# Gate-over-sum scaling of the attention's probabilities moved to GpSimd, and the order made anew

## The chip, the core and the metric

The kernel runs on one core of a Trainium2 chip. The metric is the device time of one execution in microseconds (us). Engines are named as the profile names them: PE is TensorE's matrix multiplication, PEld its weight load, DVE is VectorE, ACT is ScalarE, POOL is GpSimd, SP is SyncE, which issues the transfers.

## What is computed

One decoder block on 512 tokens of width 1024. A normalised input is projected; half of the columns go through an RWKV-7 recurrence of 8 heads, the other half through sparse attention with 8 query heads; both halves meet in an output projection, and a gated feed-forward layer and a norm follow. The attention has three branches. Two of them, the selected blocks and the window, come out for 512 tokens as two causal softmaxes over keys of their own, each weighted by a gate. Cut to what matters here:

```
gates = sigmoid(gl)                                  # (token, head, branch)
ss = einsum(q, k_sel) * scale; p_s = softmax(mask(ss))
sw = einsum(q, k_win) * scale; p_w = softmax(mask(sw))
o  = gates[0] * o_c + gates[1] * (p_s @ v_sel) + gates[2] * (p_w @ v_win)
h  = x + concat(o_rwkv, o) @ w_out
```

## The kernel before, in words

The kernel is written as a recording: methods of `Kern` call engine operations, `Program.add` keeps each as an `Op` with its buffers, and nothing is issued yet. `Program.layout` then derives who depends on whom, `Program.schedule` puts all operations of all engines into one order, and `Program.issue` (line 560 emits every instruction, so all rows of the profile have that line) writes them out in it. Each engine runs its own instructions strictly in that order. The scheduler is a list scheduler: it keeps a clock for each engine, gives each operation a duration by `Program.cost` and a rank (the longest chain of such durations behind it, plus a bonus by stage from the table `PRIO`), and starts at each step the ready operation of highest rank on the engine that is free first.

`Kern.copy` and `Program.copy` record an operation that may run on DVE or ACT; the scheduler takes the engine that would be done first. A copy with a third argument multiplies each row by a scale: on DVE it is a TENSOR_SCALAR, on ACT an ACTIVATE.

The attention (`attention`, `probs`) runs over 16 heads as the text below counts them: 4 pairs of query heads times 2 branches times 2 heads. `probs` does one of them. For each of four row tiles of 128 tokens (i = 0 to 3, with 128, 256, 384 and 512 columns of keys), PE multiplies queries and keys (two matmuls), DVE masks, scales and takes the row extreme (the profile's CUSTOM_DVE_ANT_0, ISA in the order's rows), ACT takes the exponential and the row sum. Then DVE takes the reciprocal of the four sums and multiplies it by the gate: this 128x4 factor is what the four tiles are scaled by:

```
nv.reciprocal(st[:, 3], st[:, 2])
nv.tensor_tensor(st[:, 3], st[:, 3], gt[:, :, h, br + 1], op=A.mult)
for i in range(NT):
    self.nc.copy(P[i], P[i], st[:, 3, i:i + 1])
```

In `attention` PE transposes the scaled tiles 128x128 at a time, DVE or ACT copies them out of PSUM, and PE multiplies them with the values. Three sets of tiles P (`PBUFS`) go round: a fourth head's masking waits until the first one's transpositions are done. Beside the attention PE works on the last of four RWKV pairs (`rw_chain`, a serial chain of small matmuls with a copy on DVE or ACT after each), later on the first part of the output projection (`wout`).

GpSimd only sets memory to constants in this kernel. The transfers are all issued by SP.

Of the kernel before, what the change touches and what calls it, by code (L numbers as in the profile page):

```python
# [12 lines left out]
A = mybir.AluOpType  # L13
# [58 lines left out]
def size(x):  # L72
    return math.prod(x.shape[1:])
# [115 lines left out]
class Program:  # L189
# [94 lines left out]
    def cost(self, op):  # L284

        psum = any(isinstance(x.buf.key, str) for x in op.r)
        if op.eng == "tensor":
            if op.name == "transpose":
                return size(op.w[0]) * 2 / 2.4 + 2.5
            x = op.kw["rhs"]  # L290
            n, m = size(x), size(op.kw["lhsT"])
            p = 1 if x.dtype == R32 and n >= 256 else 2 if x.dtype == R32 else 4
            return p * max(n, m) / 2.4 + (5 if n <= 128 else 105) if p == 4 else p * max(n, m) / 2.4 + 13.5
        if op.eng == "sync":
            return 475
        if op.name == "preload_act_table_set":
            return 1300
        n = max(size(x) for x in op.r + op.w)
        column = (n > 1 or op.name == "scalar_tensor_tensor") and any(size(x) == 1 for x in op.r)
        if op.eng == "scalar":  # L300
            t = 50 + 0.84 * n if psum else 94 + 0.832 * n
            return t + 93 * column + 94 * ("accum_out" in op.kw)
        if op.eng == "gpsimd":
            return 40 + 0.8 * n if op.name == "memset" else 470
        if op.name == "reciprocal":
            return 66 + 6.2 * n
        fast = op.name in ("tensor_scalar", "tensor_copy") and not psum
        return 66 + 63 * column + n / (1.92 if fast else 0.96)
# [267 lines left out]
class Kern:  # L576
# [829 lines left out]
    def probs(self, h, br):  # L1406

        self.go("probs")
        nc, at = self.nc, self.att
        nv = nc.vector  # L1410
        gt = self.gate.rearrange("p i (h b) -> p i h b", b=3)
        st = self.tl(at, [128, 4, 4], "st", bufs=3)
        P = []
        for i in range(NT):
            n = 128 * (i + 1)
            nn = max(n, 256)
            pt = self.ps("d")
            for x in range(2):
                self.mm(pt[:, :nn], self.qT[h][:, i * 128:(i + 1) * 128], self.kT[br, h // 4, x][:, :nn], x == 0, x == 1)
            pr = self.tl(at, [128, n], f"P{i}", bufs=self.PBUFS)  # L1420
            nv.tensor_tensor_reduce(pr, pt[:, :n], self.cc[:, C_CAUS + 512 - n:C_CAUS + 512], -0.125, -NEG,
                                    op0=A.add, op1=A.min, accum_out=st[:, 1, i:i + 1])
            self.act(pr, pr, AF.Exp, scale=-1.0, bias=st[:, 1, i:i + 1], accum_out=st[:, 2, i:i + 1])
            P.append(pr)
            yield
        nv.reciprocal(st[:, 3], st[:, 2])
        nv.tensor_tensor(st[:, 3], st[:, 3], gt[:, :, h, br + 1], op=A.mult)
        for i in range(NT):
            self.nc.copy(P[i], P[i], st[:, 3, i:i + 1])
        return P  # L1430

    def attention(self):
# [515 lines left out]
```

## Time and profile before

| | us |
|---|---|
| median of 3 runs | 746.78 (746.73 to 747.71) |
| the profiled execution | 746.66 |
| its span, from the first instruction to the last | 744.8 |

The profile shows that one execution. Times in it are us, counted from the start of the span. Its views are read so:
- the page's first part has, for each engine, the busy time, its share of the span and the number of instructions;
- the view by stretches has the stretch and its length, then for each engine busy us with the number of instructions, the granted share of PE's clock, the share of the DMA engines and GB/s;
- the view of waits has the engine and what it waited for: us in total, times, the longest;
- the view by forms groups instructions of one shape: engine, operation, written<-read (s is SBUF, ps is PSUM), sizes, count, busy us and mean ns of one, then idle us of that engine just before them and what ended the idle;
- the timeline has start, duration, engine, operation, sizes and count of merged rows, and in brackets idle time before them.

A matmul's duration holds its way through the array, so that rows overlap: the spacing of matmuls is less than their mean duration.

### The profile page before, as it was taken

To read this page: it belongs to the slowest core of one execution; us is meant where nothing else is said; L and a number is where in the kernel's file an instruction comes from. 1 tells how busy PE (TensorE), PEld (TensorE's weight loads), DVE (VectorE), ACT (ScalarE), POOL (GpSimd) and SP (SyncE) were. 2 spreads that over 40 slices of the span, in tenths; PEclk is the share of its full clock that TensorE was granted. 3 is DMA by queue.
4 is the path that set the end of the run, shared out by engine and by line. 5 is a ranking of instruction groups with operands and counts; after the bars stand their busy time and mean duration, and the time that the engine had idled before them with its cause. 6 is when DMAs were issued, how large, how long until landed. Compare 5 with 4: busy or idle time off the path is not lost. (4 is left out here: it accounts for less than half of the span.)

```text
span 744.8 us, 14644 instructions
## 1 busy us (share of the span) xinstructions
PE 713.2 (96%) x5540; PEld 606.7 (81%) x5540; DVE 620.0 (83%) x1480; ACT 429.9 (58%) x948; POOL 3.7 (1%) x39
## 2 busy tenths in 40 slices
PE   5999999999989989999999999999999999999996
PEld 4988975768768666666788999999999999888785
DVE  6956988986997999798538999999999994687886
ACT  6555466554554688898336566565555552533545
POOL 0000000000000000000000000000000000000000
PEclk9999999999999999999999999999999999999999
DMA  8222326202110010533311233333333307464453
GB/s 318 72 77 62 98 78 199 75 27 74 41 31 28 16 45 1 170 103 96 114 57 71 72 114 114 114 120 108 114 100 114 101 22 258 159 216 149 139 171 116
DMA packets 39829, 77.37 MB, mean 104 GB/s; under 512 B 4432, under 2 KB 8912, under 8 KB 39760
## 3 DMA queue, kind: packets, MB, share of 16 engines
q1 hardware_dynamic: 39760, 76.45, 31.5%
q8 instruction: 43, 0.70, 0.4%
q14 instruction: 26, 0.21, 0.1%
HBM read 72.24 MB, written 4.19 MB: 103 GB/s over the span
## 5 line engine op out<-in xcount | busy, mean ns | idle before, releaser
L560 PE MATMUL ps<-s,s 128*128 128x256 f32 (+11 forms) x5412 | 710.4, 304 | 25.2 <-DVE s L560 19.1
L560 PEld LDWEIGHTS ps<-s,s 128*128 128x128 f32 (+5 forms) x5412 | 604.0, 170 | 130.2 <-DVE s L560 37.9
L560 DVE TENSOR_TENSOR s<-s,s 128x512 fp32r<-128x512 f32 (+18 forms) x662 | 378.4, 607 | 38.0 <-ACT s L560 18.9
L560 ACT ACTIVATE s<-s 128x512 fp32r<-128x512 f32 (+9 forms) x395 | 237.3, 619 | 226.7 <-DVE s L560 87.0
L560 ACT ACTIVATE s<-ps 128x256 f32<-128x256 f32 (+9 forms) x286 | 103.4, 376 | 43.2 <-PE ps L560 39.7
L560 DVE TENSOR_TENSOR s<-ps,s 128x256 f32<-128x256 f32 (+5 forms) x174 | 86.2, 506 | 29.7 <-PE ps L560 28.5
L560 ACT ACTIVATE s<-s,s 128x512 f32<-128x512 f32 (+4 forms) x142 | 72.1, 526 | 26.3 <-DVE s L560 25.0
L560 DVE COPY s<-ps 128x256 f32<-128x256 f32 (+6 forms) x77 | 32.4, 429 | 6.7 <-PE ps L560 5.4
L560 DVE CUSTOM_DVE_ANT_0 s<-ps,s 128x384 f32<-128x384 f32 (+3 forms) x64 | 29.8, 484 | 3.9 <-PE ps L560 3.7
L560 DVE SCALAR_TENSOR_TENSOR s<-s,s,s 128x512 f32<-128x512 f32 (+2 forms) x32 | 19.4, 630 | 13.8 <-DMA s<-in_n1w 6.6
L560 ACT ACTIVATE s<-ps,s 128x512 f32<-128x512 f32 (+1 forms) x34 | 20.1, 621 | 12.8 <-PE ps L560 12.6
L560 DVE SCALAR_TENSOR_TENSOR s<-ps,s,s 64x64 f32<-64x64 f32 (+1 forms) x62 | 23.9, 385 | 4.1 <-PE ps L560 1.5
L560 DVE CAST s<-s 128x512 fp32r<-128x512 f32 (+6 forms) x27 | 10.9, 409 | 14.5 <-PE ps L560 10.4
L560 DVE TENSOR_SCALAR s<-s,s 128x128 f32<-128x128 f32 (+4 forms) x67 | 21.4, 353 | 1.4 <-ACT s L560 0.8
L560 DVE STREAM_SHUFFLE s<-s 128x8 f32<-128x8 f32 (+14 forms) x60 | 14.0, 234 | 0.1
L560 ACT ACTIVATION_READ_ACCUMULATOR s<-s,s 128x1 f32 x64 | 12.1, 190 | 0.0
L560 DVE SCALAR_TENSOR_TENSOR s<-s,s 128x128 f32<-128x128 f32 (+1 forms) x26 | 8.9, 347 | 0.4
L560 ACT ACT_TABLE_LOAD x6 | 7.7, 1283 | 0.8 <-PEq L1935 0.7
L560 DVE TENSOR_TENSOR_SCAN s<-s,s 128x512 f32<-128x512 f32 x4 | 4.9, 1219 | 1.9 <-ACT s L560 1.9
L560 DVE COPY s<-s 64x512 f32<-64x512 f32 (+3 forms) x16 | 5.2, 323 | 0.8 <-PE ps L560 0.5
L560 DVE CAST s<-ps 128x512 fp32r<-128x512 f32 x7 | 4.8, 682 | 0.6 <-PE ps L560 0.6
L560 DVE DVE_READ_ACCUMULATOR2_ANT s<- 128x1 f32 x64 | 5.2, 82 | 0.0
(19 smaller groups left out, 41.2 us busy)
## 6 DMA issues: line engine op xcount, KB each, us to landing
s<-in_ffn_w SPq DMA_DIRECT2D x90, 256.0 KB, 2.7
s<-in_ffn_w SPq DMA_DIRECT2D x34, 512.0 KB, 3.8
s<-in_w_in_r SPq DMA_DIRECT2D x28, 256.0 KB, 2.7
s<-in_x SPq DMA_DIRECT2D x8, 512.0 KB, 5.4
s<-in_cw SPq DMA_DIRECT2D x16, 256.0 KB, 3.3
s<-in_w_out SPq DMA_DIRECT2D x8, 512.0 KB, 3.5
s<-in_w_in_n SPq DMA_DIRECT2D x8, 256.0 KB, 2.7
scr<-s SPq DMA_DIRECT2D x4, 512.0 KB, 2.6
```

The costliest lines, as they stand in the source:

```text
L560: ins = f(*[real(x) for x in op.args], **{k: real(x) for k, x in op.kw.items()})
```

## The change

Two lines. The four scalings of each head become TENSOR_SCALAR instructions of GpSimd, in place. The scheduler's cost of a GpSimd operation that is not a memset goes from a constant to one by its columns; no other such operation stands in the kernel, so this is the cost of the scalings alone: 392, 584, 776 and 968 in its nanoseconds.

```diff
         if op.eng == "gpsimd":
-            return 40 + 0.8 * n if op.name == "memset" else 470
+            return 40 + 0.8 * n if op.name == "memset" else 200 + 1.5 * n
...
         nv.tensor_tensor(st[:, 3], st[:, 3], gt[:, :, h, br + 1], op=A.mult)
         for i in range(NT):
-            self.nc.copy(P[i], P[i], st[:, 3, i:i + 1])
+            nc.gpsimd.tensor_scalar(P[i], P[i], st[:, 3, i:i + 1], None, op0=A.mult)
         return P
```

With these the scheduler makes another order. It is the same up to the first scalings, and again from the middle of the output projection on; the order of the transfers is the same throughout.

**DVE, where the first two heads are scaled.** s_2679 and s_2684 hold the two heads' sums and factors, s_287 the gates; s_2678, s_2748, s_2931, s_3026 are the first head's four tiles, s_2753, s_2945, s_3034 three of the second's. ps_63 belongs to the RWKV chain. Before:

```order
L560 RECIPROCAL s_2679<-s_2679 128x4
L560 TENSOR_TENSOR s_2679<-s_2679,s_287 128x4
L560 TENSOR_SCALAR s_2678<-s_2678,s_2679 128x128
L560 COPY s_1207<-ps_63 128x128
L560 TENSOR_SCALAR s_3026<-s_3026,s_2679 128x512
L560 TENSOR_SCALAR s_2931<-s_2931,s_2679 128x384
L560 TENSOR_SCALAR s_2748<-s_2748,s_2679 128x256
L560 RECIPROCAL s_2684<-s_2684 128x4
L560 COPY s_947<-ps_63 64x64
L560 TENSOR_TENSOR s_2684<-s_2684,s_287 128x4
```

In the changed kernel:

```order
L560 RECIPROCAL s_2679<-s_2679 128x4
L560 TENSOR_TENSOR s_2679<-s_2679,s_287 128x4
L560 COPY s_1207<-ps_63 128x128
L560 RECIPROCAL s_2684<-s_2684 128x4
L560 TENSOR_TENSOR s_2684<-s_2684,s_287 128x4
L560 COPY s_947<-ps_63 64x64 x2
```

The chain's copies and the second head's factor move up by the scalings that stood ahead of them.

**POOL, the same two heads, in the changed kernel.** Before, nothing follows the memsets there. s_2683 is the second head's smallest tile.

```order
L560 MEMSET s_71 64x64 x4
L560 ISA
L560 TENSOR_SCALAR s_3026<-s_3026,s_2679 128x512
L560 TENSOR_SCALAR s_2931<-s_2931,s_2679 128x384
L560 TENSOR_SCALAR s_2678<-s_2678,s_2679 128x128
L560 TENSOR_SCALAR s_2748<-s_2748,s_2679 128x256
L560 TENSOR_SCALAR s_3034<-s_3034,s_2684 128x512
L560 TENSOR_SCALAR s_2945<-s_2945,s_2684 128x384
L560 TENSOR_SCALAR s_2683<-s_2683,s_2684 128x128
L560 TENSOR_SCALAR s_2753<-s_2753,s_2684 128x256
```

All 64 scalings stand in one queue, a head's four in a row, the widest first. The ISA row, which selects GpSimd's library of operations, is new too.

**PE, ahead of the fourteenth head's transpositions.** s_881 holds the keys, s_2729 and s_2733 queries of the last two heads; s_78 is the identity, so rows that read it are transpositions; s_2612 and s_2702 are parts of the output projection's left side; s_2683, s_2753, s_2945, s_3034 the fourteenth head's tiles. Before:

```order
L560 MATMUL ps_65<-s_2928,s_2651 64x512 x2
L560 MATMUL ps_62<-s_881,s_2729 128x512
L560 MATMUL ps_58<-s_881,s_2733 128x512
L560 MATMUL ps_62<-s_881,s_2729 128x512
L560 MATMUL ps_58<-s_881,s_2733 128x512
L560 MATMUL ps_61<-s_3683,s_2612 128x512
L560 MATMUL ps_59<-s_78,s_2683 128x128
L560 MATMUL ps_59<-s_78,s_2753 128x128
```

In the changed kernel:

```order
L560 MATMUL ps_63<-s_2928,s_2651 64x512 x2
L560 MATMUL ps_59<-s_881,s_2729 128x512
L560 MATMUL ps_61<-s_881,s_2733 128x512
L560 MATMUL ps_59<-s_881,s_2729 128x512
L560 MATMUL ps_61<-s_881,s_2733 128x512
L560 MATMUL ps_65<-s_78,s_3034 128x128
L560 MATMUL ps_58<-s_3614,s_2612 128x512
L560 MATMUL ps_62<-s_3631,s_2612 128x512
L560 MATMUL ps_58<-s_3631,s_2612 128x512
L560 MATMUL ps_64<-s_78,s_2945 128x128
L560 MATMUL ps_64<-s_78,s_3034 128x128
L560 MATMUL ps_60<-s_78,s_2683 128x128
```

Three output projection matmuls and the transpositions of the wider tiles now stand ahead of the first transposition of the smallest tile, where one projection matmul stood.

## Rows read from the trace of the kernel before

**Rows 1.** The page's first part: busy time by engine.
```profile
PE 713.2 (96%) x5540; PEld 606.7 (81%) x5540; DVE 620.0 (83%) x1480; ACT 429.9 (58%) x948; POOL 3.7 (1%) x39
```

**Rows 2.** View by stretches: the attention's, and one of the feed-forward layer.
```profile
270.00:366.00 96.00, 93.29 (x596) 62.24 (x596) 83.39 (x274) 78.28 (x217) 0.00 (x0) 1.00 0.28 91
...
500.00:550.00 50.00, 50.00 (x419) 50.00 (x418) 47.30 (x84) 29.23 (x59) 0.00 (x0) 1.00 0.33 106
```

**Rows 3.** Waits of PE's weight load in the stretch 270 to 366.
```profile
PEld ps L560 <- DVE s L560: 10.1, 18, 1.3
...
PEld ps L560 <- ACT s L560: 5.6, 13, 0.8
```

**Rows 4.** View by forms, 270 to 366: scaling on DVE, scaling and exponential on ACT.
```profile
L560 ACT ACTIVATE s<-s,s 128x512 f32<-128x512 f32 x22 | 15.6, 714 | 0.4 <-DVE s L560 0.3
L560 ACT ACTIVATE s<-s,s 128x384 f32<-128x384 f32 x21 | 12.4, 606 | 1.2 <-DVE s L560 1.2
...
L560 ACT ACTIVATE s<-s,s 128x128 f32<-128x128 f32 x24 | 9.3, 395 | 1.9 <-DVE s L560 1.7
L560 ACT ACTIVATE s<-s,s 128x256 f32<-128x256 f32 x17 | 8.5, 502 | 1.1 <-DVE s L560 0.9
...
L560 DVE TENSOR_SCALAR s<-s,s 128x512 f32<-128x512 f32 x10 | 4.8, 481 | 0.0
...
L560 DVE TENSOR_SCALAR s<-s,s 128x256 f32<-128x256 f32 x12 | 4.1, 346 | 0.0
L560 DVE TENSOR_SCALAR s<-s,s 128x384 f32<-128x384 f32 x9 | 3.7, 415 | 0.0
...
L560 DVE TENSOR_SCALAR s<-s,s 128x128 f32<-128x128 f32 x11 | 3.1, 282 | 0.1
```

**Rows 5.** Timeline, 344 to 346.4: the fourteenth head's factor, scalings and first transposition.
```profile
344.37 0.15 DVE L560 TENSOR_TENSOR s<-s,s 128x4 f32<-128x4 f32 x1
...
344.79 1.23 DVE L560 TENSOR_TENSOR s<-s,s 128x1024 fp32r<-128x1024 f32 x1 [0.26 <-ACT s L560]
...
345.86 0.79 ACT L560 ACTIVATE s<-s,s 128x128 f32<-128x128 f32 x2
345.93 0.81 DVE L560 TENSOR_SCALAR s<-s,s 128x512 f32<-128x512 f32 x2
...
346.30 0.33 PE L560 MATMUL ps<-s,s 128*128 128x128 f32 x1 [0.29 <-ACT s L560]
```

**Rows 6.** Timeline, 270 to 275: the first head's factor and its last three scalings.
```profile
273.12 0.17 DVE L560 TENSOR_TENSOR s<-s,s 128x4 f32<-128x4 f32 x1
...
273.73 1.07 DVE L560 TENSOR_SCALAR s<-s,s 128x512 f32<-128x512 f32 x3
```

**Rows 7.** Timeline, 343 to 353: the last two heads' factors, and their scalings on DVE.
```profile
350.28 0.24 DVE L560 TENSOR_TENSOR s<-s,s 128x4 f32<-128x4 f32 x2
350.48 1.54 DVE L560 TENSOR_SCALAR s<-s,s 128x512 f32<-128x512 f32 x5
```

**Rows 8.** View by forms, whole span: GpSimd's memsets, and DVE's scan.
```profile
L560 DVE TENSOR_TENSOR_SCAN s<-s,s 128x512 f32<-128x512 f32 x4 | 4.9, 1219 | 1.9 <-ACT s L560 1.9
...
L560 POOL MEMSET s<- 128x1 f32 x19 | 1.6, 105 | 144.4 <-DVE s L560 144.1 <-POOLq L1935 0.3
...
L560 POOL MEMSET s<- 64x64 f32 x8 | 1.2, 145 | 19.1 <-PE ps L560 18.9
```

**Rows 9.** Timeline of GpSimd, 200 to 400: its last work.
```profile
224.02 0.35 POOL L560 MEMSET s<- 64x64 f32 x2 [18.93 <-PE ps L560]
```

**Rows 10.** View by forms, 270 to 366: DVE's instructions with two SBUF inputs.
```profile
L560 DVE TENSOR_TENSOR s<-s,s 128x1024 fp32r<-128x1024 f32 x8 | 9.7, 1213 | 0.3 <-ACT s L560 0.3
...
L560 DVE TENSOR_TENSOR s<-s,s 128x512 fp32r<-128x512 f32 x9 | 5.8, 685 | 1.6 <-ACT s L560 1.0 <-PE ps L560 0.6
...
L560 DVE TENSOR_TENSOR s<-s,s 128x4 f32<-128x4 f32 x16 | 2.4, 158 | 0.1
```

**Rows 11.** Timeline, 366 to 410: PE in the output projection.
```profile
365.79 42.36 PE L560 MATMUL ps<-s,s 128*128 128x512 f32 x234
```

## Prediction

> **What bounds the kernel now.** The page's first part says where to look: PE is busy 96% of the span, DVE 83%, POOL 1% [rows 1]. So the engine that gets the work has nearly nothing to do, and the end moves only as far as PE's waits do. The view by stretches says what is special about the attention: from 270 to 366 PE is busy 93.29 of 96 us, DVE 83.39 and ACT 78.28, three engines near their limit at once, while in the feed-forward layer PE has no idle time at all [rows 2]. PE's own idle time in the stretch is therefore 96 - 93.29 = 2.7 us. The view of waits shows what lies half hidden beside it: the weight load, which runs ahead of the matmul, stood 10.1 us at 18 places until DVE, and 5.6 us at 13 places until ACT, had delivered [rows 3]. A running matmul covers part of each such wait, so 2.7 us is what PE surely loses to the two engines and 15.7 us is more than it loses.
>
> The dense stretch also gives a scale for PE's work: 419 matmuls of 256 columns in 50 us are 0.119 us apiece [rows 2]. I count others by their columns, a transposition of 128 columns in float32 like 256. Measured so, the part of PE's order that the change rearranges, some 92 us long, holds 77 us of work. The rest is mostly the change-over between small and large operands, which both orders have about as often. That is why I give the freed engines no more than a few us.
>
> **What the change removes.** 39 of the 64 scalings run on DVE (8 of the 11 instructions of 128 columns, all of the others): 8 x 0.282 + 12 x 0.346 + 9 x 0.415 + 10 x 0.481 = 15.0 us [rows 4]. The other 25 run on ACT, which has one group for them and the exponentials: 8, 4, 7 and 6 of 128 to 512 columns, 8 x 0.395 + 4 x 0.502 + 7 x 0.606 + 6 x 0.714 = 13.7 us [rows 4]. Together 28.7 of 161.7 busy us, 18% of the two engines' work in the stretch. What PE gets back lies between 0, if the waits are the RWKV chain's own length, and 6.9 us: 31 waits with 15.7 us in all [rows 3], less the 0.283 us that a matmul of 128 columns lasts, for each. I take 2.7 us, PE's idle time in the stretch: it is the nearest row, and in the new order on DVE the chain's copies and the next factor do move up.
>
> **What it adds.** Each head's four tiles, 1280 columns, now wait for four instructions of one engine in a row. No row shows POOL at such work. From below: its memsets take 105 ns for one column and 145 for 64 [rows 8], so 0.63 ns a column, and 4 x 0.105 + 1280 x 0.00063 = 1.2 us a head. From above: DVE's scan, the slowest instruction on 512 columns, takes 1.219 us [rows 8]; four of that length are 4.9 us. The nearest row in kind is ACT's, which does the same thing, one input scaled by a column: 0.395 + 0.502 + 0.606 + 0.714 = 2.2 us [rows 4]. I take that plus 0.2 us for the handing over from DVE and to PE: 2.4 us. The Trainium skill ("GPSIMD Engine Reference", Performance versus the Vector engine) gives 769 ns for a tight one-input loop of 512 elements; its 1.5 ns an element make 1.9 us for a head before any dispatch, an estimate by that page that would leave the sum as it is. No run here shows it.
>
> **What PE has in place of the wait.** What counts is how long after the factor the last tile is ready. Before, on two engines: the fourteenth head's factor was made at 344.37 + 0.15 = 344.52, but DVE then split a projection weight for 1.23 us, the first scaling began at 345.86 and the last ended at 345.93 + 0.81 = 346.74, 2.2 us later; PE had stood idle until ACT had scaled the first tile, at 346.30 [rows 5]. The first head took 1.5 us from factor to end (273.29 to 274.80) [rows 6], the last 1.5 (350.52 to 352.02) [rows 7]; over the 16 heads it is 1.65 on average, 1.0 to 2.5. On POOL it is 2.4: 0.75 us more a head. Against that stands the order: the matmuls between a head's last score and the first transposition of its smallest tile, counted by columns, hold 4.8 us on average before and 6.0 after, 1.3 us more (unrounded), because the scheduler was told of a long scaling; the fourteenth head's three projection matmuls are an example. So the point at which PE starts to wait more than before is 1.65 + 1.3 = **2.9 us a head**. At 2.4 the average head is covered. Three are not: the first and the fourteenth have gained only 0.6 us of room, and the eighth has lost 3.4 of the 7.6 that it had. I give them 1.0 us together.
>
> The rest of the edit, in one go. The scheduler's new cost does nothing of itself. POOL's queue is empty after 224.4 [rows 9] and the first factor is ready at 273.29 [rows 6], so selecting a library has 49 us; without that cover the first head would be late by its whole length. POOL's total, 16 x 2.4 = 38 us of some 80, is no bound. The transfers keep their order, and none waits for POOL. Behind the stretch, PE runs 234 projection matmuls without a gap until 408 [rows 11], so what is gained or lost before 366 arrives there whole and goes on to the end; the order there is the old one again.
>
> Sum: -2.7 + 1.0 = -1.7 us, against the profiled execution's own 746.66 (its span is 744.8, and it lies 0.12 below the median of the runs): **745.0 us**. A measurement of this kernel can tell about 0.2% from no change, 1.5 us.
>
> **Rivals.**
>
> *GpSimd is dear.* If a head costs clearly more than 2.9 us, its transpositions wait, in PE's strict order with all that stands behind them. At 3.6 us, half as much again as ACT takes and the handing over, each head is 0.7 us short; two heads are under way at a time, so that about half of the 16 waits show: 8 x 0.7 = 5.6, and -1.7 + 5.6 gives 750.6 us. At the upper bound, 4.9 us, it is 8 x 2.0 = 16, 761 us, and three sets of tiles going round would not help. For it: the whole of a head now goes through one engine, and nothing in the trace prices that. Against it: twice the taken price is needed before it becomes a matter of more than 10 us. It decides from 2.9 us a head on. Chance 0.34.
>
> *The two engines hold each other up.* DVE runs instructions with two SBUF inputs in the stretch: eight of 1.213 us, nine of 0.685, 16 of 0.158 and a few more, 20 us or a fifth of its 96 [rows 10]. If those and a scaling exclude one another, each of 64 scalings meets one with a chance of a fifth and waits 0.4 us: 5 us on POOL, 0.3 us a head, and 2.4 becomes 2.7; and DVE, meeting a POOL that is busy almost half the time, loses some 4 of the 15 us that it was freed of. The gain falls from 2.7 to 2.0 and the uncovered heads cost 2.0: no change, 746.7 us. The trace has no POOL instruction that reads, so it speaks neither way. The Trainium skill ("SBUF — State Buffer", Who interferes with whom) says that VectorE with two SBUF inputs contends with a GpSimd instruction that reads SBUF, and that the loser waits for the whole instruction. By that rule this case would be the likelier one, and it speaks against the change; no trace here can show it yet. Chance with the next one 0.28.
>
> *PE was not really waiting.* PE is busy 97% of the stretch; if the 2.7 us are the RWKV chain's own latency, nothing comes back, the scaling was hidden anyway and the three heads cost their 1.0: 747.7 us.
>
> **How the numbers follow.** Forecast, faster by 1.5 to 4 us: 0.38, and its own range is 742.8 to 745.2. No change: 0.28. Slower: 0.34, with most of it between 748.3 and 752. The range is to hold 8 in 10: it begins at 742.6, where 5 of the 6.9 us come back, which leaves out 0.06, and ends at 752.0, a price of about 3.8 us a head, which leaves out 0.13. A faster result is the likeliest single case, though slower and no change together are likelier than it.
>
> **What would show it.** In the profile of the changed kernel: 64 TENSOR_SCALAR on POOL, spaced so that four take 2.4 us (the step right) or over 2.9 (wrong); DVE's busy time in the stretch down by about 15 us or less, and ACT's by what is left when copies have changed places; PE's idle time there below 2.7 us, and its weight load waiting less for DVE and ACT. A line of the weight load waiting for POOL with over 5 us would make the first rival true; DVE's two-input forms longer than 1.213, 0.685 and 0.158 us the second; the same idle time as before the third. If the first TENSOR_SCALAR starts later than 274, selecting the library was not hidden. The forecast is wrong if PE reaches the unbroken projection run later than now, at 365.8 [rows 11].

## The result, and the profile after

The changed kernel takes 768.88 us (median of 4 runs, 767.69 to 769.30), the kernel before 747.25 beside it: 1.0278 times as long, 95% interval 1.0248 to 1.0309. The forecast was 745.0, its range ended at 752.0. Every time below is a median, with the kernel before timed beside it. Single executions, also of the kernel before, can take 5 us or more longer than the rest (753.58 beside a median of 746.93), so a profiled run can lie above its kernel's median.

The page's first part, of the changed kernel (an execution of 769.03 us):

```profile
PE 721.4 (94%) x5540; PEld 608.6 (79%) x5540; DVE 610.0 (79%) x1429; ACT 423.7 (55%) x935; POOL 74.3 (10%) x103
```

Against [rows 1] DVE has lost 10.0 us, ACT 6.2, and POOL has gained 70.6. The two engines were relieved of less than the 28.7 us of the forecast, partly because the scalings' rows overlapped (two of 0.481 and 0.415 us took 0.81 together [rows 5]); POOL took on far more than the 38 us it was given.

The view by stretches (PE, PEld, DVE, ACT and POOL busy, granted clock, DMA), once more with a longer stretch, since the last transposition comes later:

```profile
270.00:366.00 96.00, 82.14 (x496) 52.19 (x496) 63.68 (x204) 63.43 (x187) 60.74 (x55) 0.96 0.23 75
270.00:390.00 120.00, 103.61 (x604) 66.02 (x605) 72.24 (x222) 71.77 (x205) 70.60 (x64) 0.96 0.21 67
```

Where [rows 2] had three engines near their limit, no engine is near its limit now: all wait by turns. PE's idle time in the attention has gone from 2.7 us to 120 - 103.6 = 16.4. The view of waits, 270 to 390, names the engine:

```profile
PEld ps L560 <- POOL s L560: 24.2, 30, 2.5
...
PE ps L560 <- POOL s L560: 14.8, 22, 2.0
...
PEld ps L560 <- DVE s L560: 6.6, 10, 1.0
PEld ps L560 <- ACT s L560: 4.0, 7, 1.1
```

The waits for DVE and ACT did shrink, from 15.7 us [rows 3] to 10.6, as the prediction wanted; 24.2 us for POOL came in their place. POOL's view by forms (out<-in, count, busy, mean ns) and its timeline (start, length, and the idle time before it) say why:

```profile
L560 POOL TENSOR_SCALAR s<-s,s 128x512 f32<-128x512 f32 x16 | 25.5, 1599 | 82.0 <-ACT s L560 50.9 <-DVE s L560 31.0
L560 POOL TENSOR_SCALAR s<-s,s 128x384 f32<-128x384 f32 x16 | 21.4, 1339 | 0.0
L560 POOL TENSOR_SCALAR s<-s,s 128x256 f32<-128x256 f32 x16 | 14.7, 922 | 0.0
L560 POOL TENSOR_SCALAR s<-s,s 128x128 f32<-128x128 f32 x16 | 10.0, 630 | 0.0
```

```profile
289.51 4.26 POOL L560 TENSOR_SCALAR s<-s,s 128x512 f32<-128x512 f32 x4 [2.47 <-DVE s L560]
```

A head that nothing disturbs takes 4.26 us; 4.5 is the sum of the mean rows (1.599 + 1.339 + 0.922 + 0.630), and 70.6 us busy for 16 heads are 4.4. Two heads come at almost the same time, because their score matmuls stand side by side in PE's order, and queue for the one engine. The timeline around the last pair:

```profile
368.88 0.17 DVE L560 TENSOR_TENSOR s<-s,s 128x4 f32<-128x4 f32 x1
368.95 8.50 POOL L560 TENSOR_SCALAR s<-s,s 128x512 f32<-128x512 f32 x8 [1.60 <-ACT s L560]
...
374.49 10.73 PE L560 MATMUL ps<-s,s 128*128 128x128 f32 x50 [2.02 <-POOL s L560]
...
382.24 0.56 DVE L560 COPY s<-ps 128x384 f32<-128x384 f32 x1 [13.19 <-PE ps L560]
```

The second factor is ready at 369.05, the pair's scalings end at 377.45, and DVE stands idle for 13.19 us behind PE, which stands behind POOL. Before, five of the last pair's eight scalings took 1.54 us together on DVE [rows 7], and ACT did the other three.

What is lost here is lost for good. The unbroken run of projection matmuls, that ended at 365.79 + 42.36 = 408.15 [rows 11], now ends at 379.69 + 50.65 = 430.34, 22.2 us later, and the span is 22.4 longer:

```profile
379.69 50.65 PE L560 MATMUL ps<-s,s 128*128 128x512 f32 x277
```

In three stretches the granted clock is below 1.00:

```profile
270.00:282.00 12.00, 8.94 (x38) 6.28 (x39) 7.76 (x27) 9.25 (x26) 7.84 (x8) 0.86 0.07 23
330.00:342.00 12.00, 12.00 (x60) 7.55 (x61) 9.89 (x25) 7.55 (x23) 1.42 (x2) 0.86 0.32 93
366.00:378.00 12.00, 9.46 (x47) 6.29 (x48) 1.53 (x6) 2.09 (x7) 9.86 (x10) 0.86 0.00 0
```

In finer steps, for the first of them:

```profile
274.00:276.00 2.00, 0.94 (x5) 0.63 (x6) 0.72 (x5) 1.77 (x5) 1.84 (x2) 1.00 0.00 0
276.00:278.00 2.00, 1.42 (x9) 0.89 (x8) 1.59 (x4) 1.85 (x6) 2.00 (x3) 1.00 0.01 4
278.00:280.00 2.00, 1.66 (x10) 1.49 (x8) 1.56 (x7) 0.98 (x4) 2.00 (x3) 0.68 0.00 0
280.00:282.00 2.00, 2.00 (x7) 1.37 (x6) 0.92 (x3) 1.34 (x4) 2.00 (x3) 0.50 0.00 0
```

PE was busy 0.94 and 1.42 of 2 us, and then ran at the lower of its two levels, 0.50 or 1.2 GHz. On paper that is 3 x 12 x 0.14 = 5 us beside 13.7 us of added idle time, 18.7 of the 22.4; what makes the rest no row shows. Whether it is a loss of its own is the last experiment's question.

### The profile page after: what moved, and what is told of

It reads as the page before. It is cut to its first block, busy times and chain, and to the rows that moved or that the text cites. A ratio compares the mean times of both kernels' runs of the same rounds, so it can differ in the third digit from the quotient of the medians.

```text
span 767.2 us, 14723 instructions
## 1 busy us (share of the span) xinstructions
PE 721.4 (94%) x5540; PEld 608.6 (79%) x5540; DVE 610.0 (79%) x1429; ACT 423.7 (55%) x935; POOL 74.3 (10%) x103
## 5 line engine op out<-in xcount | busy, mean ns | idle before, releaser
L560 PE MATMUL ps<-s,s 128*128 128x256 f32 (+9 forms) x5412 | 718.7, 305 | 39.4 <-DVE s L560 18.3
L560 ACT ACTIVATE s<-s 128x512 fp32r<-128x512 f32 (+10 forms) x393 | 235.2, 617 | 225.3 <-DVE s L560 87.9
L560 ACT ACTIVATE s<-ps 128x256 f32<-128x256 f32 (+10 forms) x301 | 108.5, 377 | 64.8 <-PE ps L560 61.2
L560 ACT ACTIVATE s<-s,s 128x512 f32<-128x512 f32 (+4 forms) x116 | 59.8, 523 | 35.3 <-DVE s L560 34.1
L560 POOL TENSOR_SCALAR s<-s,s 128x512 f32<-128x512 f32 (+3 forms) x64 | 70.6, 1122 | 82.0 <-ACT s L560 50.9
L560 DVE CUSTOM_DVE_ANT_0 s<-ps,s 128x128 f32<-128x128 f32 (+3 forms) x64 | 30.4, 489 | 23.0 <-PE ps L560 22.1
L560 DVE COPY s<-ps 128x256 f32<-128x256 f32 (+7 forms) x62 | 27.5, 445 | 24.7 <-PE ps L560 23.3
L560 DVE SCALAR_TENSOR_TENSOR s<-s,s,s 128x512 f32<-128x512 f32 (+2 forms) x32 | 19.7, 639 | 13.7 <-DMA s<-in_n1w 6.6
L560 POOL MEMSET s<- 128x1 f32 (+3 forms) x35 | 3.5, 118 | 220.9 <-DVE s L560 180.0
L560 DVE TENSOR_SCALAR s<-s,s 128x128 f32<-128x128 f32 (+3 forms) x29 | 9.0, 329 | 1.3 <-ACT s L560 0.8
```

The costliest lines, as they stand in the source:

```text
L560: ins = f(*[real(x) for x in op.args], **{k: real(x) for k, x in op.kw.items()})
```

## Experiments

Three theories. **Price**: GpSimd takes about 4.3 us a head where the order has room for less, and PE waits. **Order**: the rearranged attention is worse, or planned with a wrong price. **Lock**: GpSimd and DVE keep each other out of SBUF, so that each one's instructions last longer.

### The order alone, and the engine alone

In the first kernel the changed order stays row by row on PE, but when it is written out the tiles of 128 and 512 columns go to DVE, the others to ACT:

```diff
+    if op.eng == "gpsimd" and op.name == "tensor_scalar":
+        if size(op.args[0]) in (128, 512):
+            op.eng = "vector"
+        else:
+            op.eng, op.name, op.args, op.kw = "scalar", "activation", (*op.args[:2], AF.Copy), dict(scale=op.args[2])
```

> The changed kernel's order, with TensorE's order the same row by row, but the scalings done by VectorE (128 and 512 columns) and ScalarE (256 and 384) as before. Price theory: the order by itself costs nothing, 744 to 751 us. Order theory (the new order of the attention part is the worse one, whoever scales): 757 us or more.

752.63 us, 1.0065 (1.0027 to 1.0102): between the two expectations, 5.3 us more than before. Not all of that need be the order's. The scalings stand in the queues of DVE and ACT where the plan had them on GpSimd, and they are split by size, while in the old order the planner had given 39 to DVE and 25 to ACT. The view of waits, 270 to 366, points to ACT, for which PEld waited 5.6 us before [rows 3] (10.3 us for DVE, 10.1 before):

```profile
PEld ps L560 <- ACT s L560: 11.9, 20, 1.4
```

I take 5.3 us as the most that the order can be blamed for; no run separates the order from the split.

The second kernel is the counterpart: the old order, all scalings planned for DVE or ACT, and then issued to GpSimd.

```diff
+    if op.tag == "scaling":
+        op.eng, (op.name, op.args, op.kw, _) = "gpsimd", op.alt["vector"]
```

> The order of the kernel before, with TensorE's order the same row by row, but all 64 scalings on GpSimd. Price theory: the order leaves about 1.65 us for what now takes 4.3, so up to 2.7 us show for each of 16 heads and more where two heads come at once: 770 to 800 us, dearer than the change itself, whose order had made some room. Order theory: 747 to 755 us, since the order is the old one.

789.81 us, 1.0567 (1.0541 to 1.0593), as price expected. The timeline begins with two heads in 8.50 us, and PE's own waits for POOL, 270 to 400, are nearly twice the 14.8 us of the change:

```profile
273.29 8.50 POOL L560 TENSOR_SCALAR s<-s,s 128x128 f32<-128x128 f32 x8 [49.23 <-DVE s L560]
```

```profile
PEld ps L560 <- POOL s L560: 34.4, 24, 3.0
PE ps L560 <- POOL s L560: 27.9, 22, 2.8
```

So the engine does the harm, and the new order, planned for GpSimd, takes half of it back (20.9 of 42.5 us).

### The plan with the true price

```diff
+        if op.eng == "gpsimd" and op.name == "tensor_scalar":
+            op.dur = 270 + 2.5 * size(op.args[0])
```

> The change with one number altered: behind the ranking, the scheduler counts a scaling on GpSimd at 270 ns + 2.5 ns a column (4.3 us for a head's four tiles, as the trace of the changed kernel has it) in place of 200 + 1.5 (2.7 us). Price theory (GpSimd takes 4.3 us a head, and there is too little other PE work to lay in between): some of the loss comes back, since the plan now knows of the wait, but not most of it: 756 to 766 us, and PEld still waits over 10 us for GpSimd in the attention. Plan theory (the loss comes of the too low price in the plan): within 3 us of the kernel before, 745 to 750 us.

765.21 us, 1.0243 (1.0200 to 1.0286): at most 3.7 us back (the intervals overlap), and PEld still waits 12.0 us for POOL, the price theory's case. A planner that knows of the wait found little to put into it.

### What any other place for the scaling could win

```diff
+            op.alt = {e: v[:3] + (0,) for e, v in op.alt.items()}
...
+    return [op for op in order if op.tag != "scaling"]
```

> The probabilities are left unscaled: the kernel before with the 64 scalings counted at nothing by the scheduler (ranks as before) and not issued, so the output lacks the factor gate over sum. This bounds what any cheaper place for the scaling could win. If VectorE and ScalarE bind the attention, as the prediction took for at most 6.9 us: 738 to 744 us. If TensorE hardly waits for them: 744.5 to 748 us, and then no engine could have made the change worth it.

744.51 us against 746.91, 0.9974 (0.9950 to 0.9999): 2.4 us, only just clear of no change. In the profiled execution (745.75 us) DVE is busy 10.9 us less in the stretch and ACT 7.2, and PE is hardly less idle:

```profile
270.00:366.00 96.00, 93.76 (x617) 63.88 (x614) 72.51 (x234) 71.08 (x203) 0.00 (x0) 1.00 0.29 95
```

96 - 93.76 = 2.24 us, against 2.7 [rows 2]. The scaling was hidden nearly whole. With this scheduler, a GpSimd that took no time at all could have won about what was forecast for a real one.

### What sets GpSimd's price

To the kernel before are added, behind the last scaling, nine GpSimd scalings and then, twice, several forms on 384 columns:

```diff
+        g.tensor_scalar(x, c, 0.5, None, op0=A.mult)
+        g.tensor_copy(x, c)
+        g.tensor_tensor(x, c, c, op=A.mult)
+        g.tensor_scalar(x, c, f, None, op0=A.mult)
+        g.memset(x, 0.0)
```

> The kernel before, and behind the last scaling of the attention 9 GpSimd multiplications of 384 columns by a per-row factor and then twice each of: multiplication by a constant, copy, product of two tiles, multiplication by a per-row factor, memset, all 128x384 into a tile nobody reads. Nobody waits for them, so the time stays within 1 per cent of before. It measures the price by form: if the per-row factor is what makes GpSimd slow, the constant and the copy take near the 0.41 us of VectorE or the 0.61 us of ScalarE; if the engine is slow at any fp32 read of SBUF, all but the memset take about 1.24 us.

The time, 754.75 us in the one run of it, missed the expectation: the tile they write lies where a later tile comes to lie, and DVE stood 13.3 us for the last memset. The rows of GpSimd while DVE did nothing, by form (L1968 with the per-row factor, L1965 with a constant):

```profile
L1968 POOL TENSOR_SCALAR s<-s,s 128x384 f32<-128x384 f32 x2 | 2.5, 1246 | 0.2
L1965 POOL TENSOR_SCALAR s<-s 128x384 f32<-128x384 f32 x2 | 2.3, 1173 | 0.2
L1967 POOL TENSOR_TENSOR s<-s 128x384 f32<-128x384 f32 x2 | 1.7, 827 | 0.2
L1966 POOL COPY s<-s 128x384 f32<-128x384 f32 x2 | 1.0, 505 | 0.1
L1969 POOL MEMSET s<- 128x384 f32 x2 | 0.8, 420 | 0.1
```

Neither expectation holds: it is not the per-row factor, and not every read. The form TENSOR_SCALAR takes 1.17 to 1.25 us, a product of two tiles 0.83, a copy 0.51. This gives a dial: the same product, cheaper.

### The cheaper form, in the changed order and in the old one

```diff
-            nc.gpsimd.tensor_scalar(P[i], P[i], st[:, 3, i:i + 1], None, op0=A.mult)
+            nc.gpsimd.tensor_tensor(P[i], P[i], st[:, 3, i:i + 1].to_broadcast(P[i].shape), op=A.mult)
```

> The changed kernel, every engine's order the same row by row, but GpSimd multiplies the tile by the factor as a second operand (TENSOR_TENSOR with the factor repeated along the columns) and not as a per-row scalar. In the run on the forms 384 columns of this form took 0.83 us where the per-row scalar took 1.25, so a head should take about 2.8 us (1280 columns by the ratio: 4.3 x 0.66), near the 2.7 us for which the order was made. Price theory: PEld's waits for GpSimd fall to a third or less of the 24 us of the changed kernel, and the time to that of its order alone and up to 5 us for what GpSimd takes from VectorE: 751 to 758 us. If what costs is the hand-over to GpSimd and back for each head: 764 us or more.

755.06 us, 1.0106 (1.0085 to 1.0128), in the range that price expected. An undisturbed head takes 2.75 us (3.1 on average: 50.0 us for 16). PEld's waits for POOL fall to 11.1 us, less than half of 24.2, though not to the third that was expected (the profiled run took 759.68 us; in the attention its clock stayed at 1.00):

```profile
298.96 2.75 POOL L560 TENSOR_TENSOR s<-s,s 128x512 f32<-128x512 f32 x4 [2.87 <-DVE s L560]
```

```profile
270.00:390.00 120.00, 112.78 (x775) 74.31 (x773) 83.87 (x249) 77.69 (x221) 50.00 (x64) 1.00 0.24 82
```

```profile
PEld ps L560 <- POOL s L560: 11.1, 19, 1.6
...
PE ps L560 <- POOL s L560: 4.5, 8, 1.4
```

In the old order, with the swap of the second kernel above:

```diff
+        op.eng, op.name, op.args, op.kw = "gpsimd", "tensor_tensor", (x, x, f.to_broadcast(list(x.shape))), dict(op=A.mult)
```

> The order of the kernel before, TensorE's order the same row by row, with all 64 scalings on GpSimd in the two-operand form. Price theory, by dose: at 4.3 us a head this order gave 789.8 us, 42.5 more than before; the old engines took 1.65 us; so at 2.8 us a head (2.8 - 1.65) / (4.3 - 1.65) = 0.43 of the 42.5 us: 760 to 770 us. If the loss is by the hand-over: 780 us or more.

761.41 us, 1.0201 (1.0171 to 1.0231): the dose again. All in one table, in us, with the time of an undisturbed head; the kernel before took 746.9 to 747.3 beside these runs:

| TensorE's order | DVE and ACT | GpSimd, 2.75 a head | GpSimd, 4.26 a head |
|---|---|---|---|
| before | 747.3 | 761.4 | 789.8 |
| changed | 752.6 | 755.1 | 768.9 |

The change's 21.6 us split at the middle column: 768.9 - 755.1 = 13.8 us come of the form TENSOR_SCALAR, with what the clock lost by its waits. POOL is busy 70.6 - 50.0 = 20.6 us longer with it, so 0.67 us show for each; in the old order it is 28.4 us for 71.4 - 46.8 = 24.6, 1.15 for each. The other 7.8 (8.1 against the kernel before timed beside) are there with the cheaper form already. The order (5.3 at most), the heads' remaining time on GpSimd and what it takes from DVE share them; no run says how.

### GpSimd beside DVE, with nobody waiting for it

```diff
+    n = (384, 384, 384, 128)[prog.turn % 4]
...
+    ins = prog.nc.gpsimd.tensor_scalar(real(x), real(prog.causal[:, :n]), real(f), None, op0=A.mult)
```

> The kernel before, order and all, with four more GpSimd multiplications behind the scaling of each head (three of 384 columns and one of 128, from a constant into a tile that nobody reads: as many columns as a head's tiles), so GpSimd works as long as in the change but nobody waits for its result. Price theory: 746 to 750 us, and VectorE's forms with two operands grow by 10 per cent at most in the attention. Lock theory (GpSimd and VectorE keep each other out of SBUF, and that is the loss): 755 us or more, with VectorE's or ScalarE's forms clearly longer than in the kernel before.

752.87 us, 1.0074 (1.0053 to 1.0095), with PE's order that of before: between the two theories, and DVE's rows, 270 to 366, are as the lock theory had them:

```profile
L560 DVE CUSTOM_DVE_ANT_0 s<-ps,s 128x512 f32<-128x512 f32 x16 | 10.8, 681 | 0.5 <-PE ps L560 0.5
...
L560 DVE TENSOR_SCALAR s<-s,s 128x256 f32<-128x256 f32 x12 | 6.8, 572 | 0.0
L560 DVE TENSOR_SCALAR s<-s,s 128x512 f32<-128x512 f32 x10 | 6.1, 611 | 0.0
...
L560 DVE TENSOR_SCALAR s<-s,s 128x384 f32<-128x384 f32 x9 | 4.7, 528 | 0.0
...
L560 DVE TENSOR_SCALAR s<-s,s 128x128 f32<-128x128 f32 x11 | 4.0, 363 | 0.1
```

DVE's TENSOR_SCALAR rows, all but three of them scalings, grew from 346, 481, 415 and 282 ns [rows 4], 15.7 us to 21.6 in all, and the scalings stand on the path of each head. The form that reads PSUM kept its length, and so did ACT's. The first row is of the kernel before, the second of this run:

```profile
L560 DVE CUSTOM_DVE_ANT_0 s<-ps,s 128x512 f32<-128x512 f32 x16 | 10.8, 684 | 0.8 <-PE ps L560 0.7
```

```profile
L560 ACT ACTIVATE s<-s,s 128x512 f32<-128x512 f32 x22 | 15.6, 713 | 0.4 <-DVE s L560 0.4
```

Then the two-operand form beside:

```diff
-    ins = prog.nc.gpsimd.tensor_scalar(real(x), real(prog.causal[:, :n]), real(f), None, op0=A.mult)
+    ins = prog.nc.gpsimd.tensor_tensor(real(x), real(prog.causal[:, :n]), real(f.to_broadcast([128, n])), op=A.mult)
```

> The kernel before with four GpSimd multiplications nobody waits for behind each head's scaling, as in the run beside, but in the two-operand form. There the one-operand form made VectorE's TENSOR_SCALAR rows 27 to 65 per cent longer and the time 5.6 us. If VectorE loses by the time GpSimd is busy: about 0.66 of that, 750 to 752 us. If VectorE loses by the columns GpSimd reads: as much or more, 753 us or more. If the two-operand form does not keep VectorE out: 746.5 to 748.5 us.

763.04 us, 1.0221 (1.0182 to 1.0260); the four runs lie between 759.79 and 768.58, and the profiled one is the shortest. That is more, though GpSimd is busy for less time (53.1 us for 76.9): the case in which VectorE loses by the columns that GpSimd reads. No run shows why.

```profile
L560 DVE TENSOR_SCALAR s<-s,s 128x256 f32<-128x256 f32 x12 | 9.6, 802 | 0.0
L560 DVE TENSOR_SCALAR s<-s,s 128x384 f32<-128x384 f32 x9 | 8.0, 887 | 0.0
L560 DVE TENSOR_SCALAR s<-s,s 128x512 f32<-128x512 f32 x10 | 7.8, 784 | 0.0
```

So the lock's effect is real, and it costs a kernel that scales on DVE as well. The change itself scales nothing there, and the common forms left to it grew little: its 128x1024 product from 1213 ns [rows 10] to 1267, the 128x4 one from 158 to 173. Two rarer ones grew more: the third here from 742, and four TENSOR_SCALAR of 128 columns that scale something else from 282 to 431.

```profile
L560 DVE TENSOR_TENSOR s<-s,s 128x1024 fp32r<-128x1024 f32 x8 | 10.1, 1267 | 0.1
...
L560 DVE TENSOR_TENSOR s<-s,s 128x4 f32<-128x4 f32 x14 | 2.3, 173 | 0.2
...
L560 DVE SCALAR_TENSOR_TENSOR s<-s,s,s 128x512 f32<-128x512 f32 x2 | 1.8, 894 | 0.0
```

With the cheaper form in the changed order the 128x4 product took longer still, so the 13.8 us that this form won were not won by a weaker lock:

```profile
L560 DVE TENSOR_TENSOR s<-s,s 128x4 f32<-128x4 f32 x16 | 4.1, 263 | 0.2
```

### A part of the work, and more tiles

Only the smallest tile on GpSimd, planned at its true price:

```diff
+            nc.gpsimd.tensor_scalar(P[i], P[i], st[:, 3, i:i + 1], None, op0=A.mult) if i == 0 else self.nc.copy(P[i], P[i], st[:, 3, i:i + 1])
```

> Of each head only the tile of 128 columns is scaled by GpSimd, counted at 270 ns + 2.5 ns a column; the other three go to VectorE or ScalarE by the old rule. Price theory: 0.63 us of GpSimd lies beside the 0.9 us that the two other engines need for the three other tiles, so nobody waits for GpSimd much and the loss is gone: 745 to 750 us. If a hand-over to GpSimd costs by the head and not by the column: 755 us or more.

747.05 us, 1.0003 (0.9979 to 1.0027): no change, as price expected. But one tile took 916 ns on GpSimd where the change's took 630: beside a DVE that scales, GpSimd is held up as well.

```profile
L560 POOL TENSOR_SCALAR s<-s,s 128x128 f32<-128x128 f32 x16 | 14.6, 916 | 111.8 <-ACT s L560 61.6 <-DVE s L560 40.2 <-PE ps L560 9.9
```

The two smallest tiles, in the two-operand form:

```diff
+            nc.gpsimd.tensor_tensor(P[i], P[i], st[:, 3, i:i + 1].to_broadcast(P[i].shape), op=A.mult) if i < 2 else self.nc.copy(P[i], P[i], st[:, 3, i:i + 1])
```

> Of each head the tiles of 128 and 256 columns are scaled by GpSimd in the two-operand form (counted at 200 ns + 1.5 ns a column), the other two by VectorE or ScalarE. With the scalings left out altogether the time was 2.4 us under that of before, so nothing here can win more: price theory 744.5 to 749 us, as with the smallest tile alone. If GpSimd's two-operand form keeps VectorE out of SBUF for its whole length: 750 us or more.

748.70 us, 1.0020 (0.9998 to 1.0042): not to be told from before. A fourth set of tiles, with the true price in the plan:

```diff
-    PBUFS, PTBUFS, TB = 3, 3, 22
+    PBUFS, PTBUFS, TB = 4, 2, 22
```

> The change with the true price in the plan (as in the run of that name) and four sets of probability tiles in place of three (the transposed tiles have two sets in place of three, which makes the room), so that a head's scaling can be spread over more of the others' work. If the loss is latency that more tiles can cover: 750 to 758 us. If it is lack of other TensorE work in the attention while GpSimd takes 4.3 us for each head (16 x 4.3 = 69 us of the stretch), or the sets of the transposed tiles are missed: 762 us or more.

762.70 us, 1.0218 (1.0169 to 1.0268). Beside 765.21 with three sets (intervals overlap) more tiles help little or not at all. None of these versions beat the kernel before, and the run without scalings says why.

### The waits filled

```diff
+            for k in range(8):
+                ins = prog.nc.tensor.transpose(real(op.args[0]), real(prog.ident), real(prog.ident))
```

> The changed kernel with eight more TensorE transpositions (of a constant, into columns that the next transposition overwrites; 0.109 us each, 0.87 us in all) in front of 16 of the transpositions before which TensorE stood for 0.6 to 2.2 us in its trace; GpSimd, VectorE and ScalarE do just what they did. In the changed kernel the granted clock fell to 0.5 to 0.7 three times in the attention, each time behind such waits. If that part of the loss comes of the waits by way of the clock: the clock stays at 1.00 from 270 to 390 us and the time falls by 2 to 6 us, to 763 to 767 us, though TensorE has 14 us more to do. If the clock's fall has another cause, or costs nothing: 768 us or more, by up to the 14 us.

768.41 us, 1.0280 (1.0253 to 1.0308). The clock did as the expectation's first case wanted, the time as its second:

```profile
270.00:390.00 120.00, 113.74 (x737) 77.47 (x738) 72.85 (x223) 72.21 (x205) 70.52 (x64) 1.00 0.22 69
...
330.00:342.00 12.00, 11.95 (x72) 7.21 (x71) 10.64 (x27) 8.66 (x26) 2.68 (x3) 1.00 0.36 110
366.00:378.00 12.00, 10.44 (x66) 7.04 (x64) 1.53 (x6) 2.33 (x6) 9.50 (x10) 1.00 0.00 0
```

With work put into the waits the granted clock stayed at 1.00, so its falls did come of the waits. The time stayed where it was. PE's timeline at the last pair, where the change stood 2.02 us until 374.49:

```profile
371.94 1.03 PE L1965 MATMUL ps<-s 128*128 128x128 f32 x8
374.12 1.14 PE L560 MATMUL ps<-s,s 128*128 128x128 f32 x5 [1.15 <-POOL s L560]
```

Eight added transpositions fit into the wait, and it still ends when POOL delivers, at 374.12. At such a place a slow clock only fills time in which PE would wait. Elsewhere, 16 times about 1 us of added work may have cost what the clock gave back; this run does not tell the two apart, so how much of the 5 us on paper is a loss of its own stays open.

## Why the prediction was wrong

- **What bounds the kernel: right, and taken too lightly.** PE's 2.7 us of idle time were read rightly. That all of it would come back took the most that could be won for the value: with no scaling at all 2.4 us come back in the time, and PE's idle time shrinks by 0.5. The third rival, that PE was not really waiting, was nearly true of the scalings.
- **What it adds: the step that failed.** "The nearest row in kind is ACT's ... 2.4 us" a head. POOL's rows give 4.26 undisturbed and 4.4 on average, near the upper bound of 4.9. A row of the same operation on another engine was no measure: by form GpSimd's own prices differ by a factor of 2.5 (0.51 us for a copy, 1.25 for this scaling), and nothing in the trace of before told which it would be. Bounds four times apart deserved more than 0.34 for the dear half.
- **The break-even point of 2.9 us a head: wrong as well.** With the cheaper form a head takes 2.75 us, 3.1 on average, so that by the prediction's rule next to nothing should be lost. The same order is 8.1 us slower than before, and PEld still waits 11.1 us for POOL. Two heads share one queue (8.50 us for a pair at the full price), which a room counted for each head leaves out. Part of that room may also be the way through DVE and ACT to the factor; no run shows that. And the sum took the new order for a gain in room alone, where it may itself cost up to 5.3 us.
- **The first rival was the case**, by its own sign (24.2 us of PEld's waits, where it asked for 5) and its own condition. Its rule that "about half of the 16 waits show" is not far off as a slope in the changed order, where 0.67 of each added us shows (1.15 in the old one). Its level was too low: at 4.4 us a head it would give 746.7 - 1.7 + 8 x 1.5 = 757, since it started from a gain of 1.7 us where, at 3.1 us a head, 8.1 us were lost.
- **The second rival** was real but not the main cause here: the forms that it named grew by 4 and 9 per cent. It named DVE's two-input forms alone, while the one that suffers most has one tile as its input, and the change took that one away. The Trainium skill ("SBUF — State Buffer", Who interferes with whom) lists the one-input scaling among the forms that can, under conditions on their operands, take the pair of ports that DVE shares with GpSimd, and says that ACT waits for nobody. The runs agree: 346 ns became 572 beside GpSimd, and ACT's 128x512 rows kept their 714 ns [rows 4] (713 there).
- **The library** was hidden, though the first scaling began at 274.16, past the 274 that was to tell: its factor had come later too, at 273.66 + 0.17 = 273.83. The hand-over from DVE took 0.33 us, where 0.2 was reckoned for both sides.
- **Behind the stretch** the prediction held: 22.2 us at the end of the projection, 22.4 in the span.

## What to carry to other kernels

An idle engine is no free engine: what counts is how long one piece takes there on the way that others wait for, and the change moved 1.65 us of it to 4.3 and more. Before moving work, take it away altogether: that run, 2.4 us, showed at once that there was next to nothing to win. And when an operation has no row on the engine that is to do it, time its forms there, beside what the other engines do, since the form alone made a factor of 1.5 here.

## What the runs showed of the hardware

- On GpSimd 384 float32 columns took 0.42 us as a memset, 0.51 as a copy, 0.83 as a product of two tiles and 1.17 to 1.25 as TENSOR_SCALAR. The Trainium skill ("GPSIMD Engine Reference", Performance versus the Vector engine) has 769 ns for 512 elements of a tight loop and 4497 ns for a 2048-element sum of two tiles. By proportion, an estimate, that is 0.58 and 0.84 us for 384: the product agrees, the copy is a little faster, and the TENSOR_SCALAR took twice the first, so that the page's figure is no price for it. The prediction's estimate by it, 1.9 us a head, stands against 4.26 measured.
- GpSimd's two-operand form lengthened DVE's scalings more (346 to 802 ns at 256 columns) than the one-operand form (to 572), though it was busy for a third less time. DVE's rows that read PSUM kept their length beside both (681 ns for 512 columns, 684 before). GpSimd's 128-column scaling took 630 ns in the change and 916 beside a DVE that scales too.
- TensorE's granted clock fell to 0.50, 1.2 GHz, after it had been busy 0.94 and 1.42 of 2 us, and did not fall when such waits were filled with transpositions whose result nobody used.
